# Chunk 5's phased convolution taps between the two halves of the last output pair, and chunk 7's VectorE taps less tied to chunk 6

## The chip, the cores and the metric

One core of a Trainium2 chip runs the whole program. The core has a matrix engine (TensorE, PE in the profile), three elementwise engines (VectorE or DVE, ScalarE or ACT, GpSimd or POOL) and queues that issue transfers: nearly all loads are issued, in order, by SP's queue, a few by ACT's. The metric is the time of one execution on the device, in microseconds, as a median over several executions. Each engine works through its own instruction list in order and waits on semaphores where an operand or a buffer isn't ready.

## The reference

The program is a two-layer decoder trunk in float32 on 512 tokens of 1024 channels. Layer 0 has a causal Conformer convolution module, layer 1 differential attention; each is followed by a SwiGLU feed-forward part and a gated per-layer embedding. Only the convolution module of layer 0 matters here:

```
a = x @ w_pw1 + b_pw1                       # 1024 -> 2048
u = a[..., :1024] * sigmoid(a[..., 1024:])
u = depthwise causal conv of u over 31 tokens, per channel, + dw_b
u = silu(layer_norm(u, ln_g, ln_b))
h = x + u @ w_pw2 + b_pw2
```

## The kernel before, in words

**Tiling.** Channels are cut into 8 chunks of 128, one chunk to the 128 partitions, with the 512 tokens along the free side. A float32 product is made of three matmuls on a high and a low part of each operand (lines 167 to 169), so one half of an output pair, which sums over 8 chunks of the input, is 24 matmuls of 128x512.

**Output pairs.** The loop over c makes, for each chunk, a pair of halves: the gate half `pg` and the linear half `pa`. VectorE scales both by the norm's row (line 583 for the gate, line 589 for the other), ScalarE takes the sigmoid (line 584), and VectorE multiplies them to the convolution's input (line 595 for phased chunks, line 603 for the others).

**Three ways to make the 31 taps.** A tap is a shifted copy of the input times one weight per channel.
- Chunks 1, 3, 5 and 6 are phased: the input goes to DRAM (line 420) and back (line 424, four loads) so that four tokens in four phases lie on the partitions, and 72 matmuls of 128x128 (line 457) with prepared matrices make all taps. The matrices come by line 437 (groups 0 and 1), line 443 (groups 2 and 3) and line 447 (the last lag of all groups). Then ScalarE copies the sum out (line 465), it goes to DRAM (line 467, ACT's queue) and back in token order (line 470, four loads on SP's queue), and VectorE adds the bias and the shift (line 475): the chunk's output y.
- Chunks 0, 2 and 4 are done by VectorE (lines 505 and 508) and, for some taps, by ScalarE's products and GpSimd's sums (lines 495 and 496).
- Chunk 7 is done by all: 8 taps on TensorE (line 413, matrices by line 412), 7 by ScalarE and GpSimd (lines 492, 495, 496), 16 on VectorE (one at line 505 and 15 at line 508). VectorE adds the three at lines 512 and 514.

**Moments.** For the layer norm, every chunk's y is added to a sum (line 543) and its square (ScalarE, line 536) to another (line 541). After the last chunk, TensorE sums over the channels (line 198, four groups of matmuls), and a short chain over VectorE, GpSimd and ScalarE makes the norm's factors, which the second linear layer waits for. Between these stand products of the per-layer embedding (`factor`, 6 matmuls of 128x512 each), which need nothing of the convolution.

**What sets the order.** The program is written in one order, and an automatic scheduler then lists each engine's instructions by its own simulated times; `issue_after(x)` holds an instruction's place in the list behind that of x. Two tables say at which pair a chunk's phased taps are written: `BETWEEN[c]` puts them between the two halves of pair c, `BEHIND[c]` behind its second half.

```
        if c > 0:
            pg = half(wg) if c > 1 else g1
            for k in BETWEEN[c]:
                pe_taps(k)
            pa = half(wa) if c > 1 else a1
            for k in BEHIND[c]:
                pe_taps(k)
```

Tiles have fixed homes: a new tile waits until its home's last user is done. The matrices of phased chunks live in D0 to D5 (one buffer each) and C5 (two). Chunk 6 uses D3 and D4 for its group 0, D5 for the last lag, D0 and D1 for group 1; chunk 5 uses D0 and D1, D2, then D3 and D4; chunk 7's TensorE taps use D2 and D3.

Of the kernel before, what the change touches and what calls it, by code (L numbers as in the profile page):

```python
# [26 lines left out]
KW = 31  # L27
# [31 lines left out]
PHASED = (1, 3, 5, 6)  # L59


BETWEEN = ((), (0,), (), (1, 2), (), (3, 4), (), ())
BEHIND = ((), (), (), (), (), (), (5,), (6,))
NPH = 4
FG = P // NPH
LAGS = (KW + NPH - 2) // NPH + 1
# [25 lines left out]
def trunk(ctx, tc, xT, xtok, pT, wts, diag, dww, vec, rel, onehot, lamv, out):  # L92
# [9 lines left out]
    def sb(shape, tag, bufs, dt=F32):  # L102
        uid[0] += 1
        return pool.tile(shape, dt, tag=tag, name=f"{tag}_{uid[0]}", bufs=bufs)
# [17 lines left out]
    def col(name, i=0):  # L122
        a, _ = VEC[name]
        return vt[:, a + i : a + i + 1]
# [260 lines left out]
    last_shift = [None]  # L385
# [4 lines left out]
    def half(w):  # L390
        acc = mm()
        for k in range(NC):
            mm3(acc, wpart(w, k), norm.u[k], k == 0, k == NC - 1)
        return acc

    def wt(c, j):
        return dwt[:, c * KW + j : c * KW + j + 1]
# [4 lines left out]
    def pe_taps(c):  # L402

        acc = accs[c] = sc() if c < NC - 2 else mm()
        if c in PHASED:
            return phased_taps(c, acc)
        for j in range(PE_TAPS[c]):
            if j % 4 == 0:
                n = min(4, PE_TAPS[c] - j)
                dg = sb([P, 4, P], f"D{2 + j // 4}", 1)  # L410
                with after_weights(c):
                    nc.sync.dma_start(dg[:, :n], diag[TAPS.index((c, j)), :, :n])
            last_tap[0] = T.matmul(
                acc, dg[:, j % 4], ups[c][:, j : j + S], start=(j == 0), stop=(j == PE_TAPS[c] - 1)
            )
# [46 lines left out]
    def phased_out(c):  # L462

        o = big()
        last_out[0] = A.copy(o, accs[c])
        d = dram.tile([P, S], F32, tag=f"po{c}", name=f"po{c}")
        nc.scalar.dma_start(d, o)
        both_ = sb([P, 2, S], f"B{c}", 1)
        for g in range(NPH):
            nc.sync.dma_start(  # L470
                both_[g * FG : (g + 1) * FG, 1].rearrange("p (r n) -> p r n", r=NPH),
                bass.AP(d.tensor, d.offset + g * P, [[S, FG], [FG * S, NPH], [1, P]]),
            )
        tok = "p (n r) -> p n r"
        last_shift[0] = V.scalar_tensor_tensor(
            both_[:, 0].rearrange(tok, r=NPH), both_[:, 1].rearrange("p (r n) -> p n r", r=NPH), col("dw_b", c),
            shrow.rearrange(tok, r=NPH), ALU.add, ALU.add,
        )
        y[c] = both_[:, 0]

    def other_taps(c):
        if c in PHASED:
            return phased_out(c)
        up, acc = ups[c], accs[c]
        alone = c in ALONE
        tap = lambda j: up[:, j : j + S]
        a, b = PE_TAPS[c], PE_TAPS[c] + POOL_TAPS[c]
        pacc = wk()
        for j in range(a, b):
            if j == a:  # L490
                with tc.issue_after(last_out[0].ins) if alone else nullcontext():
                    A.activation(pacc, tap(j), AF.Identity, scale=wt(c, j), bias=col("dw_b", c))
            else:
                pr = sb([P, S], f"C{2 + j % 2}", 2)
                A.activation(pr, tap(j), AF.Copy, scale=wt(c, j))
                G.tensor_tensor(pacc, pacc, pr, ALU.add)  # L496
        yc = sb([P, 2, S], f"B{c}", 1)
        if c == 0:
            sums["acc"] = yc[:, 1]
        yc = yc[:, 0]  # L500
        sum_ = sc() if alone else acc
        if c == 0:
            V.tensor_scalar(sum_, tap(b), wt(c, b), None, ALU.mult)
        else:
            V.scalar_tensor_tensor(sum_, tap(b), wt(c, b), shrow, ALU.mult, ALU.add)
        for j in range(b + 1, KW):
            with tc.issue_after(last_shift[0].ins) if alone and j == KW - 4 else nullcontext():
                last_v_tap[0] = V.scalar_tensor_tensor(sum_, tap(j), wt(c, j), sum_, ALU.mult, ALU.add)  # L508
        if alone:
            moments(NC - 2)  # L510
        with tc.issue_after(last_sum[0].ins) if alone else nullcontext():
            V.tensor_tensor(yc, sum_, pacc, ALU.add)
        if alone:
            last_add[0] = V.tensor_tensor(yc, acc, yc, ALU.add)
        y[c] = yc
# [10 lines left out]
    def moments(c):  # L526
        if c == 0:
            t = tp()
            T.matmul(t, ones, y[0], start=True, stop=True)
            A.activation(shrow, t, AF.Copy, scale=-1.0 / P)  # L530
            V.scalar_tensor_tensor(y[0], t, -1.0 / P, y[0], ALU.mult, ALU.add)
            A.activation(sums["acc"], y[0], AF.Square)
            return
        sq = sums["sq"] = wk()
        with tc.issue_after(last_factor[0].ins) if c > NC - 3 else nullcontext():
            A.activation(sq, y[c], AF.Square)
        if c == NC - 1:
            return
        eng, at = (V, tc.issue_after(last_v_tap[0].ins)) if c == NC - 2 else (G, nullcontext())
        with at:  # L540
            last_sum[0] = eng.tensor_tensor(sums["acc"], sums["acc"], sq, ALU.add)
            if c > 1:
                eng.tensor_tensor(macc, y[1] if c == 2 else macc, y[c], ALU.add)
# [6 lines left out]
    for c in range(NC):  # L550
# [24 lines left out]
# [7 lines that stand above are left out]
# [18 lines left out]
        else:  # L600
            up = ups[c] = sb([P, S + PAD], "C0", 2)
            G.memset(up[:, :PAD], 0.0)
            V.scalar_tensor_tensor(up[:, PAD:], ta, col("b_pw1", c), tg, ALU.add, ALU.mult)
        for k in BETWEEN[c] + BEHIND[c]:
            other_taps(k)
# [22 lines left out]
    for m in range(5):  # L628
        factor(last_tap)
        if m == 1:  # L630
            last_factor[0] = last_copy[0]
    other_taps(NC - 1)
    moments(NC - 1)

# [838 lines left out]
```

## Time and profile before

| | us |
|---|---|
| median of 3 runs | 1249.22 |
| lowest and highest of them | 1247.81 and 1250.43 |
| the profiled execution's own time | 1246.65 |
| its span (first to last instruction) | 1244.8 |
| TensorE busy in it | 1231.8 |
| VectorE, ScalarE, GpSimd busy | 879.8, 623.7, 464.7 |

The profiled execution is 2.57 us faster than the median, and 1.85 us of it lie outside its span. Times in the profile count from the span's start. In a list of waits a row names who waited, for whom, the microseconds in total, how often, and the longest. In a timeline a row gives start, length, engine, line, what is written from what, and in brackets the idle time before it with what ended it. Buffer numbers are left out there.

### The profile page before, as it was taken

Reading aid. Unit: us, or ns where it says so; the run is one execution under the profiler, and the core shown is the slowest. Engines: PE = TensorE matmul, PEld = TensorE weight load, DVE = VectorE, ACT = ScalarE, POOL = GpSimd, SP = SyncE. Lnnn points to the kernel's source line nnn. Section 1 sums busy time; section 2 is a strip of 40 time slices with the busy share of each in tenths; the row PEclk is TensorE's granted clock in tenths of the full one; section 3 lists DMA queues with packets and bytes.
Section 4 is the critical chain, followed back from the end, with each engine's and each line's share of the span. In section 5 each row is a group of like instructions: output and inputs, shape, how many; then the busy total and the mean of one; then the engine's idle time right before and its main releaser. Section 6 shows DMA issues by size and latency. Waiting matters only on the chain.

```text
span 1244.8 us, 18364 instructions
## 1 busy us (share of the span) xinstructions
PE 1231.8 (99%) x7048; PEld 1078.6 (87%) x7048; DVE 879.8 (71%) x1244; ACT 623.7 (50%) x1098; POOL 464.7 (37%) x351
## 2 busy tenths in 40 slices
PE   9999999999999999999999999999999999999998
PEld 7887788888998899888888888788889998999887
DVE  5997866985895479547676876646966885588535
ACT  7742464433553255435666877735434552455432
POOL 0953442024670464133436645041026650552120
PEclk9999999999999999999999999999999999999999
DMA  9756214234233322334332331142233333232331
GB/s 328 226 179 189 82 54 121 92 98 127 88 100 118 102 86 78 109 104 153 130 116 63 112 94 34 52 150 87 90 127 90 103 113 111 83 102 86 105 98 68
DMA packets 50019, 138.44 MB, mean 111 GB/s; under 512 B 5731, under 2 KB 10851, under 8 KB 49932
## 3 DMA queue, kind: packets, MB, share of 16 engines
q1 hardware_dynamic: 47664, 133.71, 34.1%
q10 hardware_dynamic: 2268, 3.57, 1.0%
q8 instruction: 55, 0.90, 0.3%
q14 instruction: 32, 0.26, 0.1%
HBM read 130.94 MB, written 6.31 MB: 110 GB/s over the span
## 4 chain that ended last, share of the span: by engine, by line
PE 84%; DVE 7%; issue 4%; ACT 2%; POOL 2%; DMA 1%; SPq 0%; DVEq 0%; POOLq 0%; ACTq 0%
PE mm L167 26%; PE mm L168 25%; PE mm L169 25%; DVE wlo L782 2%; POOL wk L496 1%; PE mm L1188 1%; DVE sc L508 1%; DVE wlo L162 1%; PE sc L457 1%; PE sc L1155 1%; PE sc L1156 1%; DVE B L873 1%; PE mm L457 1%; PE tp L1175 1%; PE tp L1109 1%
## 5 line engine op out<-in xcount | busy, mean ns | idle before, releaser
L160 ACT CAST whi<-wraw 128x1024 fp32r<-128x1024 f32 (+1 forms) x139 | 141.2, 1024 | 219.8 <-PE mm L169 110.3
L162 DVE TENSOR_TENSOR wlo<-wraw,whi 128x1024 fp32r<-128x1024 f32 (+1 forms) x135 | 174.2, 1296 | 81.9 <-ACT whi L160 81.1
L167 PE MATMUL mm<-A,wlo 128*128 128x512 f32 (+1 forms) x552 | 214.0, 388 | 0.1
L168 PE MATMUL mm<-A,whi 128*128 128x512 f32 (+1 forms) x552 | 213.4, 387 | 0.0
L169 PE MATMUL mm<-A,whi 128*128 128x512 f32 (+1 forms) x552 | 211.0, 388 | 0.0
L167 PE MATMUL mm<-B,wlo 128*128 128x512 f32 x352 | 137.0, 389 | 0.0
L168 PE MATMUL mm<-B,whi 128*128 128x512 f32 x352 | 137.0, 389 | 0.0
L169 PE MATMUL mm<-B,whi 128*128 128x512 f32 x352 | 135.6, 389 | 0.0
L228 POOL TENSOR_TENSOR acc<-acc,wk 128x512 f32<-128x512 f32 x35 | 60.3, 1724 | 189.8 <-ACT wk L227 189.2
L168 PE MATMUL mm<-C,whi 128*128 128x256 f32 x448 | 126.8, 283 | 0.0
L167 PE MATMUL mm<-C,wlo 128*128 128x256 f32 x448 | 126.8, 283 | 0.0
L169 PE MATMUL mm<-C,whi 128*128 128x256 f32 x448 | 126.8, 283 | 0.0
L169 PEld LDWEIGHTS mm<-A,whi 128*128 128x128 f32 x552 | 103.6, 188 | 22.3 <-DVE A L206 1.1
L167 PEld LDWEIGHTS mm<-A,wlo 128*128 128x128 f32 x552 | 103.8, 188 | 21.7 <-DVE h L1319 0.5
L168 PEld LDWEIGHTS mm<-A,whi 128*128 128x128 f32 x552 | 103.8, 188 | 20.5
L782 DVE TENSOR_TENSOR wlo<-A,whi 128x1024 fp32r<-128x1024 f32 x60 | 107.5, 1802 | 19.7 <-ACT whi L781 19.7
L781 ACT CAST whi<-A 128x1024 fp32r<-128x1024 f32 x60 | 62.9, 1048 | 54.6 <-PE mm L169 43.8
L791 POOL TENSOR_TENSOR A<-wraw 128x512 f32<-128x512 f32 x16 | 23.7, 1482 | 169.8 <-DMA wraw<-in_wts 147.0
L791 POOL TENSOR_TENSOR A<-A 128x512 f32<-128x512 f32 x16 | 24.6, 1536 | 165.3 <-DMA A<-in_wts 162.6
L168 PEld LDWEIGHTS mm<-C,whi 128*128 128x128 f32 x448 | 86.0, 192 | 0.2
L167 PEld LDWEIGHTS mm<-C,wlo 128*128 128x128 f32 x448 | 86.0, 192 | 0.2
L169 PEld LDWEIGHTS mm<-C,whi 128*128 128x128 f32 x448 | 86.0, 192 | 0.0
(324 smaller groups left out, 3057.1 us busy)
## 6 DMA issues: line engine op xcount, KB each, us to landing
wraw<-in_wts SPq DMA_DIRECT2D x159, 512.0 KB, 3.6
A<-in_wts SPq DMA_DIRECT2D x32, 512.0 KB, 3.6
wraw<-in_wts SPq DMA_DIRECT2D x16, 384.0 KB, 3.1
D<-in_diag SPq DMA_DIRECT2D x22, 256.0 KB, 4.5
C<-in_diag SPq DMA_DIRECT2D x16, 256.0 KB, 4.7
h<-in_xT SPq DMA_DIRECT2D x8, 256.0 KB, 4.7
B<-in_xtok SPq DMA_DIRECT2D x4, 512.0 KB, 7.2
rest<-h SPq DMA_DIRECT2D x8, 256.0 KB, 2.6
```

Source lines behind the costliest of these rows:

```text
L160: A.copy(hi[:, cut], raw[:, cut])
L162: eng.tensor_tensor(lo[:, cut], raw[:, cut], f(hi[:, cut]), ALU.subtract)
L167: T.matmul(acc, al, bh, start=first, stop=False, **kw)
L168: T.matmul(acc, ah, bh, start=False, stop=False, **kw)
L169: return T.matmul(acc, ah, bl, start=False, stop=last, **kw)
L228: self.last = self.eng.tensor_tensor(self.acc, self.acc, sq, ALU.add)
L457: last_tap[0] = T.matmul(acc[:, g * P : (g + 1) * P], w, ups[c][:, g, LEAD - m : LEAD - m + P], start=(m == 0), stop=(m == LAGS - 1),)
L496: G.tensor_tensor(pacc, pacc, pr, ALU.add)
L508: last_v_tap[0] = V.scalar_tensor_tensor(sum_, tap(j), wt(c, j), sum_, ALU.mult, ALU.add)
L781: A.copy(hi, src)
L782: V.tensor_tensor(lo, src, f(hi), ALU.subtract)
L791: G.tensor_tensor(s[:, 0], r1[:, 0], r1[:, 1], ALU.add)
```

## The change

Chunk 5's phased taps leave the place behind pair 6 and are written between the two halves of pair 7. Of chunk 7's 15 taps at line 508, formerly the last four were held behind chunk 6's shift (line 475); now only the last one is.

```
-BETWEEN = ((), (0,), (), (1, 2), (), (3, 4), (), ())
-BEHIND = ((), (), (), (), (), (), (5,), (6,))
+BETWEEN = ((), (0,), (), (1, 2), (), (3, 4), (), (5,))
+BEHIND = ((), (), (), (), (), (), (), (6,))
...
         for j in range(b + 1, KW):
-            with tc.issue_after(last_shift[0].ins) if alone and j == KW - 4 else nullcontext():
+            with tc.issue_after(last_shift[0].ins) if alone and j == KW - 1 else nullcontext():
                 last_v_tap[0] = V.scalar_tensor_tensor(sum_, tap(j), wt(c, j), sum_, ALU.mult, ALU.add)
```

Here is what the scheduler makes of it at three places. The first is TensorE around the start of chunk 5's taps. `sc_1003` and `sc_1047` are chunk 5's sum before and now, `mm_1085` and `mm_1022` the gate half of pair 7. Before:

```order
L169 MATMUL mm_1085<-A_33_141,whi_942 128x512
L167 MATMUL mm_1085<-A_34_146,wlo_943 128x512
L168 MATMUL mm_1085<-A_34_146,whi_942 128x512
L457 MATMUL sc_1003<-C_162_867,D_187_1004 128x128 x4
L457 MATMUL sc_1003<-C_162_867,D_188_1006 128x128 x4
L457 MATMUL sc_1003<-C_162_867,D_189_1008 128x128
```

Now:

```order
L167 MATMUL mm_1022<-A_40_172,wlo_943 128x512
L168 MATMUL mm_1022<-A_40_172,whi_942 128x512
L169 MATMUL mm_1022<-A_40_172,whi_942 128x512
L457 MATMUL sc_1047<-C_162_867,D_193_1048 128x128 x4
L457 MATMUL sc_1047<-C_162_867,D_194_1050 128x128 x4
L457 MATMUL sc_1047<-C_162_867,D_195_1052 128x128
```

The scheduler had let 5 of the gate half's 24 matmuls go ahead of chunk 5's taps; now all 24 do, and the 72 taps follow, and then the linear half of pair 7 and chunk 6's taps as before. The number of matmuls is the same.

The second place is VectorE from chunk 4's last sum (line 512) to chunk 6's shift (the last row). `B_199` and `B_213` are chunk 5's output before and now, `B_215` chunk 6's; `sc_1306` is chunk 7's sum. Before:

```order
L512 TENSOR_TENSOR B_176_915<-sc_832,wk_883 128x512
L583 TENSOR_TENSOR big_1188<-mm_1085,rb_273 128x512
L475 SCALAR_TENSOR_TENSOR B_199_1075<-B_199_1075,vec_63,shrow_190 128x512
L589 TENSOR_TENSOR big_1189<-mm_1110,rb_273 128x512
L603 SCALAR_TENSOR_TENSOR C_213_1194<-big_1189,vec_63,big_1188 128x512
L505 SCALAR_TENSOR_TENSOR sc_1306<-C_213_1194,C_31_133,shrow_190 128x512
L508 SCALAR_TENSOR_TENSOR sc_1306<-C_213_1194,C_31_133,sc_1306 128x512 x11
L475 SCALAR_TENSOR_TENSOR B_215_1201<-B_215_1201,vec_63,shrow_190 128x512
```

Now:

```order
L512 TENSOR_TENSOR B_176_915<-sc_832,wk_883 128x512
L589 TENSOR_TENSOR big_1179<-mm_1100,rb_273 128x512
L603 SCALAR_TENSOR_TENSOR C_211_1184<-big_1179,vec_63,big_1178 128x512
L505 SCALAR_TENSOR_TENSOR sc_1306<-C_211_1184,C_31_133,shrow_190 128x512
L508 SCALAR_TENSOR_TENSOR sc_1306<-C_211_1184,C_31_133,sc_1306 128x512 x5
L475 SCALAR_TENSOR_TENSOR B_213_1191<-B_213_1191,vec_63,shrow_190 128x512
L508 SCALAR_TENSOR_TENSOR sc_1306<-C_211_1184,C_31_133,sc_1306 128x512 x8
L475 SCALAR_TENSOR_TENSOR B_215_1201<-B_215_1201,vec_63,shrow_190 128x512
```

Chunk 5's shift has moved from ahead of pair 7's linear half into the middle of chunk 7's taps; the gate half's line 583 has moved ahead of line 512, among chunk 4's taps. Two taps instead of four stand behind chunk 6's shift.

The third place is SP's queue, from the write of chunk 6's input to chunk 5's return. `D_204`, `D_205`, `D_207`, `D_208` and the C tiles by line 443 are chunk 6's matrices before; `D_202`, `D_203` (its group 0), `D_205`, `D_206` (group 1) and `C_207`, `C_208` are the same ones now. `D_225` and `D_226` are for chunk 7's TensorE taps. Before:

```order
L437 DMA D_207_1142<-in_diag 128x512
L420 DMA pi_1063<-big_1061 128x512
L437 DMA D_208_1144<-in_diag 128x512
L156 DMA wraw_1452<-in_wts 128x1024
L437 DMA D_204_1136<-in_diag 128x512
L424 DMA C_197_1065<-pi_1063 32x4x128 x4
L437 DMA D_205_1138<-in_diag 128x512
L443 DMA C_209_1146<-in_diag 128x512 x2
L443 DMA C_210_1149<-in_diag 128x512 x2
L412 DMA D_225_1228<-in_diag 128x512
L470 DMA B_199_1075<-po_1073 32x4x128 x4
L412 DMA D_226_1234<-in_diag 128x512
```

Now:

```order
L420 DMA pi_1010<-big_1008 128x512
L156 DMA wraw_1452<-in_wts 128x1024
L424 DMA C_189_1012<-pi_1010 32x4x128 x4
L437 DMA D_205_1132<-in_diag 128x512
L437 DMA D_206_1134<-in_diag 128x512
L437 DMA D_202_1126<-in_diag 128x512
L437 DMA D_203_1128<-in_diag 128x512
L443 DMA C_207_1136<-in_diag 128x512 x2
L443 DMA C_208_1139<-in_diag 128x512 x2
L412 DMA D_225_1228<-in_diag 128x512
L412 DMA D_226_1234<-in_diag 128x512
L470 DMA B_213_1191<-po_1189 32x4x128 x4
```

Chunk 6's four D matrices now stand together behind the four loads of its input, group 1's ahead of group 0's, and chunk 5's return stands behind both loads for chunk 7. On ScalarE's list, which is not shown, chunk 5's copy (line 465) stood ahead of the square of chunk 4's output (line 536) and now stands behind it; the write to DRAM (line 467) follows the first of chunk 7's products (line 495); and the square of chunk 5's output stands directly ahead of chunk 6's copy (line 465) and of chunk 7's line 492.

## Prediction

> **What bounds the kernel now.** I read the page's busy times first (TensorE 1231.8 of a span of 1244.8 us), then the list of what TensorE waited for over the whole program, largest first:
>
> ```profile
> PE sc L457 <- DMA C<-pi: 3.0, 1, 3.0
> PE tp L142 <- POOL ident masks.py:199: 1.5, 1, 1.5
> ...
> PE tp L660 <- ACT wk L657: 0.7, 1, 0.7
> ```
>
> TensorE is the bound nearly everywhere, and its longest single wait is the one at phased taps (line 457) for an input that comes back from DRAM. So I asked next where that wait stands: TensorE's timeline around it.
>
> ```profile
> 100.66 0.39 PE L167 MATMUL mm<-A,wlo 128*128 128x512 f32 x1
> ...
> 101.56 0.39 PE L168 MATMUL mm<-A,whi 128*128 128x512 f32 x1
> 104.90 0.55 PE L457 MATMUL sc<-C,D 128*128 128x128 f32 x1 [2.95 <-DMA C<-pi]
> ...
> 114.49 0.48 PE L169 MATMUL mm<-A,whi 128*128 128x512 f32 x1
> ...
> 118.91 0.39 PE L167 MATMUL mm<-A,wlo 128*128 128x512 f32 x1
> ...
> 124.35 4.18 PE L457 MATMUL mm<-C,D 128*128 128x128 f32 x36
> ...
> 132.38 7.04 PE L413 MATMUL mm<-C,D 128*128 128x512 f32 x16
> ```
>
> It is chunk 5, behind the five gate matmuls that start at 100.66 to 101.56; 19 more of that half stand ready behind the waiting taps. The wait costs more than its length, as windows show (length, TensorE's busy time and its matmuls, granted clock, share and rate of the transfers):
>
> ```profile
> 101.90:104.90 3.00, 0.05 (x1) 0.98 0.78 150
> 104.90:106.00 1.10, 1.10 (x5) 0.50 0.59 194
> ...
> 107.00:108.00 1.00, 1.00 (x6) 0.50 0.01 4
> 108.00:109.00 1.00, 1.00 (x11) 0.92 0.71 227
> ...
> 154.00:155.00 1.00, 1.00 (x4) 1.00 0.00 0
> ```
>
> After the gap the clock is at half until about 108. After the 0.7 us gap at 153 (third row of the waits) it stays at 1.00.
>
> **What the change takes away.** Matmuls of 512 columns start 0.227 us apart (118.91 to 124.35 for 24 of them), so the taps could have begun at 101.56 + 0.23 = 101.79 and began at 104.90: 3.11 us. Chunk 5's 72 taps take 114.49 - 104.90 = 9.59 us, chunk 6's equal 72 take 132.38 - 124.35 = 8.03 us: 1.56 us more for the half clock. With the whole gate half ahead, the taps start at 101.79 + 19 x 0.227 = 106.1, later than the 104.9 at which their input was there, without a gap: **4.67 us** go. The matmuls are the same in number. TensorE then stands 4.67 us earlier at the linear half (end 119.8 for 124.5), at chunk 6's taps (119.7 for 124.35) and onward, if nothing else is late.
>
> [...]
>
> **What must come earlier now.** Three chains are less covered than before.
>
> *Chunk 6's input and matrices.* SP's queue, and times to landing (last number) of single transfers from 110 to 113 us:
>
> ```profile
> 110.07 0.33 SPq L420 DMA_DIRECT2D pi<-big  x1
> ...
> 111.12 0.33 SPq L156 DMA_DIRECT2D wraw<-in_wts  x1
> ...
> 112.11 1.75 SPq L424 DMA_DIRECT2D C<-pi  x4
> ```
>
> ```profile
> D<-in_diag SPq DMA_DIRECT2D x1, 256.0 KB, 2.6
> wraw<-in_wts SPq DMA_DIRECT2D x1, 512.0 KB, 5.3
> D<-in_diag SPq DMA_DIRECT2D x1, 256.0 KB, 6.3
> C<-pi SPq DMA_DIRECT2D x1, 64.0 KB, 6.0
> ```
>
> VectorE's list up to line 595 is unchanged, so the write of chunk 6's input stays at 110.07 and its loads at 112.11 to 113.9. They landed by about 119.5 (113.5 + 6.0) with 1 MB queued ahead (two D tiles of 256 KB and one weight); now the weight alone, 0.5 MB, is ahead: I take about 117.5. The four D loads follow from 113.9, the one needed last for group 0 behind the weight's landing, with which it shares a semaphore (111.12 + 5.3 at most): issued by 116 at the latest, needed at 119.7 + 4 x 0.11 = 120.1. The two D rows bound its landing: 2.6 us gives 118.6 and no wait, 6.3 gives 122.3 and a wait of 2.2 us. The queue is shorter than that of the 6.3 row and longer than that of the 2.6 row; I take a wait of 0.2 us. Groups 2 and 3 have 4 us more.
>
> *Chunk 5's return.* VectorE's timeline, in which chunk 5's shift is the row of 126.15:
>
> ```profile
> 126.15 1.12 DVE L475 SCALAR_TENSOR_TENSOR B<-B,vec,shrow 128x512 f32<-128x512 f32 x1 [6.35 <-DMA B<-po]
> 127.19 0.68 DVE L589 TENSOR_TENSOR big<-mm,rb 128x512 f32<-128x512 f32 x1
> ...
> 129.28 1.66 DVE L505 SCALAR_TENSOR_TENSOR sc<-C,C,shrow 128x512 f32<-128x512 f32 x1
> 130.97 8.67 DVE L508 SCALAR_TENSOR_TENSOR sc<-C,C,sc 128x512 f32<-128x512 f32 x11
> 139.68 1.85 DVE L475 SCALAR_TENSOR_TENSOR B<-B,vec,shrow 128x512 f32<-128x512 f32 x1
> ...
> 146.46 0.69 DVE L514 TENSOR_TENSOR B<-mm,B 128x512 f32<-128x512 f32 x1
> ```
>
> VectorE stood 6.35 us before chunk 5's shift and held the linear half of pair 7 (line 589) behind it, 2.7 us after TensorE had ended it. Now line 589 runs at 119.9 and line 505 at 119.9 + 2.1 = 122.0. From line 505 to the end of line 514 the old list took 147.15 - 129.28 = 17.87 us; the new one has the same work and chunk 5's shift in it, 1.12: 141.0, if neither return is waited for. The returns:
>
> ```profile
> 127.36 0.63 ACT L536 ACTIVATE wk<-B 128x512 f32<-128x512 f32 x1 [4.69 <-DVE B L475]
> ...
> 132.59 0.59 ACT L465 COPY big<-mm 128x512 f32<-128x512 f32 x1 [0.74 <-PE mm L457]
> 133.07 0.81 ACT L492 ACTIVATE wk<-C,vec,C 128x512 f32<-128x512 f32 x1
> 133.20 0.33 ACTq L467 DMA_DIRECT2D po<-big  x1
> ```
>
> ```profile
> 122.68 1.75 SPq L470 DMA_DIRECT2D B<-po  x4
> ...
> 135.19 1.75 SPq L470 DMA_DIRECT2D B<-po  x4
> ```
>
> Chunk 5's copy now stands on ScalarE behind chunk 4's square and its write behind chunk 7's first product, which needs line 603: it goes out at about 122.6. Chunk 6's write took 135.19 - 133.20 = 2.0 us to landing, so chunk 5's loads go at 124.7, also past the load for chunk 7's D3, which waits only for chunk 6's first taps (121). Chunk 5's shift began 126.15 - 122.68 = 3.5 us after its loads: now 128.2. Line 505 and five taps of 0.79 us end at 127.65, so VectorE waits 0.5 us.
>
> *Chunk 6's return and chunk 7's sum.* Behind chunk 5's shift (end 129.3) ScalarE's list has that chunk's square (0.63, line 536), then chunk 6's copy (0.59): the write goes at 130.5, the loads at 132.5, and landing 4.3 us after (139.5 for 135.19 as the upper bound, since VectorE didn't wait there) gives 136.8, against eight taps that end at 135.6: 1.2 us. So chunk 7's output comes at 141.0 + 0.5 + 1.2 = 142.7. GpSimd's six sums are behind the same copy:
>
> ```profile
> 127.41 1.28 POOL L543 TENSOR_TENSOR acc<-acc,B 128x512 f32<-128x512 f32 x1 [5.84 <-DVE B L475]
> 128.65 1.74 POOL L541 TENSOR_TENSOR B<-B,wk 128x512 f32<-128x512 f32 x1
> 133.96 8.67 POOL L496 TENSOR_TENSOR wk<-wk,C 128x512 f32<-128x512 f32 x6 [3.58 <-ACT wk L492]
> ```
>
> Line 492 ends at 131.3, chunk 5's two moments on GpSimd (1.28 + 1.74) at 132 to 132.4, and 132.4 + 8.67 = 141.1 is in time for line 512 (141.2). TensorE asks for chunk 7's output here:
>
> ```profile
> 147.87 1.06 PE L198 MATMUL sc<-ones,B 128*128 128x128 f32 x8
> ```
>
> That was 0.7 us after it was ready; now it asks at 147.87 - 4.67 = 143.2, 0.5 us after 142.7. The cover is thin: if the returns are as quick as chunk 5's, the wait is 0; if both are slow, several us (the rivals). I take 0.3 us.
>
> Behind these sums every list is the old one and starts from TensorE, so the rest moves as a block. Sum: 4.67 - 0.2 - 0.3 = 4.2 us. The profiled execution of 1246.65 (span 1244.8 and 1.85 around it) would take 1242.5; the median shown lies 2.57 above the profiled execution, and from it the forecast is **1245.0**.
>
> **The rivals.**
>
> *The half clock isn't paid in every execution.* The runs lie between 1247.81 and 1250.43, more than 1.56 apart, so the profile may not show the usual case. Then 3.11 - 0.5 = 2.6 us go: 1246.6. For it: the gap is the only one of its length, so the trace has no second case. Against it: the profiled execution paid it and was the fastest of the four. [...]
>
> *Chunk 6's matrices become the new wait.* The D row of 6.3 us gives 2.2 us: 4.67 - 2.2 - 0.3 = 2.2, so 1247.0. For it: six 256 KB loads and the input now go out in one block. Against it: 0.5 MB less is queued ahead of the input.
>
> *Chunk 7's sum eats the gain.* A lateness of 1.5 to 3 us beyond 143.2 leaves nothing to 3 us: about 1248.5.
>
> *Slower: the two returns follow each other.* Chunk 6's copy now waits for chunk 5's shift, by ScalarE's order, so slow transfers add up. Slow rows of their kinds:
>
> ```profile
> po<-big ACTq DMA_DIRECT2D x1, 256.0 KB, 4.1
> B<-po SPq DMA_DIRECT2D x1, 64.0 KB, 4.3
> ```
>
> With 4.1 for both writes, 4.3 behind the last issue for the first return and 6.0 (the row of C<-pi, same size and kind) for the second: chunk 5's shift at 126.7 + 1.3 + 4.3 = 132.3, chunk 6's write at 134.6, its last load landing at 138.7 + 1.3 + 6.0 = 146.0, and from there 5.9 (the old 147.15 - 139.68 less two taps) make 152. TensorE would wait 8.8 us and then run at half clock for 1.56 more: 10.4 - 4.67 = 5.7 slower, 1254.9. It decides from a lateness of 3.1 us, where 3.1 + 1.56 equals the gain. Against it: these rows are from the crowded stretches, and traffic around 125 to 136 is light.
>
> **How the numbers follow.** Chances: forecast 0.58 (own range 1243.6 to 1246.2), half clock not usual 0.12, matrices 0.15, gain eaten 0.09, slower 0.06. A difference of 0.2%, 2.5 us, is about what a measurement of this kernel can tell from no change, so faster means below 1246.7: all of the forecast and two thirds of the two cases behind it, whose waits reach down to none, 0.76; same 0.18; slower 0.06. The range reaches from 1243.2 (no waits at all, 1244.6, and the spread of a median) to 1247.9, beyond the matrices' case, and leaves out most of the last two.
>
> **What would show it.** Right: no wait of TensorE at chunk 5's taps, 72 of them in 8.0 us from about 106.1, granted clock 1.00 throughout 100 to 160, pair 7's linear half ending near 119.8, chunk 5's shift near 128, line 198 starting near 141.4 instead of 146.08. Wrong: a wait at chunk 6's taps for D or C<-pi; a wait at line 198 for line 514; or a difference that arises behind 155, where I expect none.

## The result, and the profile after

| kernel | median, us | lowest to highest | runs |
|---|---|---|---|
| before | 1248.80 | 1247.54 to 1250.71 | 6 |
| changed | 1243.91 | 1243.17 to 1245.44 | 6 |

The change makes the kernel faster by 4.9 us: the ratio is 0.9963, with a 95% interval of 0.9952 to 0.9975. The prediction was 1245.0, in a range of 1243.2 to 1247.9. The profiled execution of the changed kernel is the slowest of its six, 1245.44 us with a span of 1243.6, while that of the kernel before, 1246.65, was quicker than each of its six timed runs. So the two traces must be compared by what happens in them and not by their ends: 1243.6 against 1244.8 looks like 1.2 us.

The list of what TensorE waited for in the changed kernel, between 95 and 165 us:

```profile
PE sc L457 <- DMA C<-pi: 1.3, 1, 1.3
PE mm L457 <- DMA D<-in_diag: 1.2, 1, 1.2
PE tp L660 <- ACT wk L657: 1.2, 1, 1.2
```

The wait of 3.0 us at chunk 5's taps is 1.3 now, a wait for chunk 6's matrices is new, and the third one, for the factors of the norm, grew from 0.7 to 1.2. TensorE's timeline gives their places (chunk 5's taps, chunk 6's taps, chunk 7's taps, the first and the third sum of the moments):

```profile
108.00 4.26 PE L457 MATMUL sc<-C,D 128*128 128x128 f32 x36 [1.26 <-DMA C<-pi]
...
122.94 4.26 PE L457 MATMUL mm<-C,D 128*128 128x128 f32 x36 [1.20 <-DMA D<-in_diag]
...
131.05 7.04 PE L413 MATMUL mm<-C,D 128*128 128x512 f32 x16
...
144.74 1.05 PE L198 MATMUL sc<-ones,acc 128*128 128x128 f32 x8
...
146.56 1.16 PE L198 MATMUL sc<-ones,B 128*128 128x128 f32 x8
```

In the trace of before, chunk 5's taps and the first sum stood here:

```profile
104.90 5.81 PE L457 MATMUL sc<-C,D 128*128 128x128 f32 x36 [2.95 <-DMA C<-pi]
...
146.08 1.05 PE L198 MATMUL sc<-ones,acc 128*128 128x128 f32 x8
```

The first 36 records of either chunk's taps take 4.26 us now; chunk 5's took 5.81 at half clock. The windows around chunk 5's taps (length, TensorE's busy time, the busy times of its weight loads and the other engines, and then the granted clock) show that the short gap no longer slows what follows:

```profile
107.00:108.00 1.00, 0.00 (x1) 0.03 (x1) 0.00 (x0) 0.00 (x0) 0.00 (x0) 1.00 0.77 181
108.00:109.00 1.00, 1.00 (x9) 1.00 (x10) 0.71 (x1) 0.00 (x0) 0.00 (x0) 1.00 0.84 332
109.00:110.00 1.00, 1.00 (x12) 1.00 (x11) 1.00 (x2) 0.56 (x2) 0.45 (x1) 1.00 0.16 61
```

Why is there a gap at all, with the whole gate half ahead of the taps? SP's queue tells it: the write of chunk 5's input, its loads, the write of chunk 6's input, its loads, and four matrices.

```profile
99.10 0.33 SPq L420 DMA_DIRECT2D pi<-big  x1
...
102.58 1.80 SPq L424 DMA_DIRECT2D C<-pi  x4
...
113.16 0.34 SPq L420 DMA_DIRECT2D pi<-big  x1
...
115.19 2.53 SPq L424 DMA_DIRECT2D C<-pi  x4
117.82 1.80 SPq L437 DMA_DIRECT2D D<-in_diag  x4
```

In the execution of before, the loads of chunk 5's input were issued at 100.16 and chunk 6's input was written at 110.07; here it is 102.58 and 113.16, although nothing ahead of them was changed. This execution ran about 2.4 to 3.1 us late there. VectorE's timeline shows the same, at the shifts of chunks 3, 5 and 6 (line 475) and chunk 7's last sum (line 514):

```profile
108.29 1.12 DVE L475 SCALAR_TENSOR_TENSOR B<-B,vec,shrow 128x512 f32<-128x512 f32 x1 [1.81 <-DMA B<-po]
...
131.53 1.11 DVE L475 SCALAR_TENSOR_TENSOR B<-B,vec,shrow 128x512 f32<-128x512 f32 x1 [1.47 <-DMA B<-po]
...
139.64 1.85 DVE L475 SCALAR_TENSOR_TENSOR B<-B,vec,shrow 128x512 f32<-128x512 f32 x1 [0.79 <-DMA B<-po]
...
145.82 0.69 DVE L514 TENSOR_TENSOR B<-mm,B 128x512 f32<-128x512 f32 x1
```

The first of these, chunk 3's shift, stood here in the trace of before:

```profile
105.20 1.11 DVE L475 SCALAR_TENSOR_TENSOR B<-B,vec,shrow 128x512 f32<-128x512 f32 x1 [1.14 <-DMA B<-po]
```

It began at 105.20 before and at 108.29 here, 3.09 us later; all the same, line 198 begins at 144.74 instead of 146.08. From chunk 3's shift, which lies ahead of everything the change touches, to line 198 it is 146.08 - 105.20 = 40.88 us before and 144.74 - 108.29 = 36.45 now: **4.43 us less**. I use this distance as a yardstick for the runs below, since it takes an execution's own lateness out. It is one execution of each kernel, and where TensorE has slack it absorbs some of that lateness; it is a reading aid, and the verdicts go by the timed runs.

The stall on VectorE went the same way. It stood 6.35 us before chunk 5's shift, with pair 7's product behind it; now 1.47.

### The profile page after: what moved, and what is told of

The parts are those of the page before. It is cut to its first block, busy times and chain, and to the rows that moved or that the text cites. A ratio compares the mean times of both kernels' runs of the same rounds, so it can differ in the third digit from the quotient of the medians.

```text
span 1243.6 us, 18365 instructions
## 1 busy us (share of the span) xinstructions
PE 1230.1 (99%) x7048; PEld 1077.2 (87%) x7048; DVE 879.4 (71%) x1244; ACT 624.8 (50%) x1098; POOL 467.5 (38%) x351
## 4 chain that ended last, share of the span: by engine, by line
PE 84%; DVE 7%; DMA 4%; issue 3%; ACT 1%; SPq 0%; POOL 0%; ACTq 0%; DVEq 0%
PE mm L167 26%; PE mm L168 26%; PE mm L169 26%; DMA wraw<-in_wts 2%; DVE wlo L162 2%; PE mm L1188 1%; DVE sc L508 1%; DVE wlo L782 1%; PE sc L1155 1%; PE sc L1156 1%; DMA B<-in_xtok 1%; PE tp L1175 1%; PE mm L457 1%; PE tp L1109 1%; PE mm L413 1%
## 5 line engine op out<-in xcount | busy, mean ns | idle before, releaser
L791 POOL TENSOR_TENSOR A<-wraw 128x512 f32<-128x512 f32 x16 | 26.3, 1643 | 165.8 <-DMA wraw<-in_wts 143.4
```

The lines of the kernel that those rows point to most:

```text
L791: G.tensor_tensor(s[:, 0], r1[:, 0], r1[:, 1], ALU.add)
```

## The experiments

All were timed beside the kernel before on the same chip, in four groups. The kernel before lies between 1247.35 and 1248.57 in them, so ratios are compared rather than medians of different groups. The ratios are as the comparison of each group gives them and not the quotient of the two medians.

| run | median, us | lowest to highest, runs | before beside it | ratio, 95% interval |
|---|---|---|---|---|
| e1 tables only | 1246.26 | 1244.17 to 1248.33, 12 | 1248.57 | 0.9982, 0.9972 to 0.9991 |
| e2 hold only | 1247.80 | 1245.91 to 1250.14, 11 | 1248.57 | 0.9998, 0.9989 to 1.0007 |
| e3 filled gap | 1247.50 | 1246.68 to 1248.85, 11 | 1248.57 | 0.9996, 0.9987 to 1.0006 |
| e3b short fill | 1247.45 | 1245.90 to 1248.74, 11 | 1247.38 | 1.0002, 0.9994 to 1.0011 |
| e3c fill and order | 1247.33 | 1245.66 to 1248.45, 11 | 1247.35 | 0.9997, 0.9988 to 1.0006 |
| e11 fill and hold | 1247.12 | 1245.38 to 1248.60, 12 | 1248.05 | 0.9994, 0.9985 to 1.0003 |
| e4 group 0 first | 1243.99 | 1243.00 to 1244.62, 5 | 1248.57 | 0.9967, 0.9955 to 0.9978 |
| e5 write first | 1243.16 | 1241.97 to 1244.21, 8 | 1247.38 | 0.9970, 0.9960 to 0.9980 |
| e7 products early | 1242.39 | 1240.31 to 1242.55, 6 | 1247.38 | 0.9964, 0.9952 to 0.9976 |
| e8 shift late | 1241.25 | 1240.77 to 1241.79, 5 | 1247.38 | 0.9959, 0.9947 to 0.9971 |
| changed, again | 1243.49 | 1242.25 to 1244.29, 5 | 1247.35 | 0.9965, 0.9953 to 0.9978 |
| e8, again | 1241.72 | 1240.72 to 1242.57, 5 | 1247.35 | 0.9952, 0.9938 to 0.9965 |

### The two edits apart

e1 moves the taps and keeps the old hold:

```
-BETWEEN = ((), (0,), (), (1, 2), (), (3, 4), (), ())
-BEHIND = ((), (), (), (), (), (), (5,), (6,))
+BETWEEN = ((), (0,), (), (1, 2), (), (3, 4), (), (5,))
+BEHIND = ((), (), (), (), (), (), (), (6,))
```

> Only chunk 5's taps are moved between the halves of pair 7; the last four of chunk 7's VectorE taps stay held behind chunk 6's shift, so the shift stands after 11 of the 15 taps instead of 13. In the changed kernel's trace that shift waited 0.79 us for its return with 13 taps ahead, and chunk 7's output was ready when TensorE asked for it. Theory (the move of the taps brings the gain, and the cover of chunk 7's sum is used up): the shift waits 0.79 + 2 x 0.79 = 2.4 us, chunk 7's output is up to 1.6 us later, TensorE waits about 1.2 us at line 198: 1243.9 + 1.2 = 1245.1, still 3.7 below the kernel before. Rival (chunk 7's sum has cover to spare, the hold is idle): 1243.9.

e2 keeps the tables and changes the hold:

```
-            with tc.issue_after(last_shift[0].ins) if alone and j == KW - 4 else nullcontext():
+            with tc.issue_after(last_shift[0].ins) if alone and j == KW - 1 else nullcontext():
```

> Only the hold is loosened (the shift of chunk 6 after 13 of chunk 7's taps instead of 11), chunk 5's taps stay behind pair 6. In the trace of before VectorE did not wait at that shift, and TensorE not at line 198. Theory: no change, 1248.8 within 1. Rival (the loosened hold brings a good part of the gain by itself): 1246 or less.

The hold alone gives nothing (0.9998). The tables alone give 0.9982, about half of the whole change's 0.9963, and the two intervals (0.9972 to 0.9991 and 0.9952 to 0.9975) hardly overlap: taken across the two groups, about 2 us are left for the hold once the taps have moved. I had expected a wait of 1.2 us at line 198 in e1 and 1245.1 us; line 198 did not wait there, and the time was 1246.26. TensorE in e1, chunk 5's taps and chunk 6's:

```profile
106.67 4.18 PE L457 MATMUL sc<-C,D 128*128 128x128 f32 x36
...
122.44 5.88 PE L457 MATMUL mm<-C,D 128*128 128x128 f32 x36 [2.11 <-DMA C<-in_diag]
```

No wait at chunk 5's taps: the gap of before is gone, as the prediction's first step has it. The half clock has moved: a wait of 2.11 us for matrices and then 5.88 us for the 36 records at chunk 6's taps. VectorE in e1, chunk 6's shift:

```profile
139.73 1.70 DVE L475 SCALAR_TENSOR_TENSOR B<-B,vec,shrow 128x512 f32<-128x512 f32 x1 [3.84 <-DMA B<-po]
```

VectorE stands 3.84 us before that shift with four taps of chunk 7 and four sums behind it; with the new hold two of these four taps run ahead of the shift. With the old order (e2) VectorE has no wait there to fill, so the same edit does nothing. That this is how the hold gains is argued and not shown: VectorE's sum of line 543 ended at 145.06 in e1, before line 198 began at 145.89, and what TensorE lost up to there it lost at chunk 6's taps. Part of e1's distance is that half clock: its four runs with a mean clock of 0.998 average 1247.2 us, the eight others 1245.4, and none of the changed kernel's eleven is below 0.999. Whether the hold keeps the clock up there was not tried. By the yardstick e1 gains only 40.88 - (145.89 - 106.13) = 1.1 us in its profiled execution.

e2's profile holds the gap of before in a larger size:

```profile
106.08 5.88 PE L457 MATMUL sc<-C,D 128*128 128x128 f32 x36 [3.96 <-DMA C<-pi]
```

### Is the half clock a cost of its own?

e3 keeps the order of before and lets TensorE do idle work in the gap, so that the clock stays up (1.00 there in its profile). The product of the filler is thrown away.

```
+FILL = 27
...
+                    started[0] = mm()
+                    with tc.manual_schedule(engines={T.engine}):
+                        for n in range(5):
+                            gate_matmul(pairs[NC - 1][1], n)
+                        fill = tp()
+                        for _ in range(FILL):
+                            T.matmul(fill[:, 0:P], ident, ones, start=True, stop=True)
+                        pe_taps(k)
```

> The kernel before with 27 matmuls of 128x128 that nobody reads between the fifth gate matmul of pair 7 and chunk 5's taps: about 3.0 us of work in the gap, so that the wait stays and only the idleness goes. The matmuls, their operands and VectorE's list are those of before; on SP's queue chunk 6's D matrices move behind its input, where they have 5 us to spare. Theory (the half clock behind the gap costs 1.56 us in the usual execution): 1248.8 - 1.5 = 1247.3, 72 taps in 8.0 us, granted clock 1.00 at 100 to 115. Rival (the profiled execution was unusual there, and the wait alone is the price): 1248.8, with the taps as long as before in only some executions.

The size was wrong: a float32 matmul of 128x128 stands twice in the records, at 0.11 us each, so 27 of them took 6.19 us, longer than the gap. (So the 72 that stand for a chunk's taps are records too, of 36 matmuls in the program.) The clock was 1.00 from 100 to 160 and the ratio 0.9996, which tells nothing of the half clock's price. e3b has `FILL = 14`.

> The kernel before with 14 matmuls of idle work (recorded as 28, some 3.1 us by the 0.1115 us of a record in the run with the longer filler) put ahead of chunk 5's phased taps, where TensorE waited 2.95 to 3.96 us for their input. The filler's product is thrown away. My theory, that the half clock behind that gap is a cost of its own of about 1.5 us which goes when the gap is filled: no stretch below clock 1.00 at 105 to 110, the 36 first records of taps in about 4.2 us rather than 5.9, and 1247.1 us beside 1248.6 for the kernel before. Rival, that the half clock does not occur in most executions, or that what comes behind the taps waits anyway: 1248.6, within 0.2% of the kernel before.

The 28 records took 3.29 us, no stretch from 100 to 160 was below 1.00, the first 36 taps took 4.26 us and chunk 6's taps began at 123.61 instead of 124.35. The total did not move (1.0002). In its profile ScalarE's copy of chunk 5's sums stood behind chunk 4's square, at 120.36 instead of 114.77, and chunk 7's taps waited 1.27 us. e3c takes that away by holding the square behind the write:

```
-        with tc.issue_after(last_factor[0].ins) if c > NC - 3 else nullcontext():
+        held = last_factor[0] if c > NC - 3 else outs[c + 1] if c == 4 else None
+        with tc.issue_after(held.ins) if held else nullcontext():
             A.activation(sq, y[c], AF.Square)
```

> The kernel before with the short filler again, and with chunk 4's square on ScalarE held behind the write to DRAM of chunk 5's sums. In the first run with the short filler no stretch was at half clock and chunk 6's taps began at 123.61 us rather than 124.35, but ScalarE's copy of chunk 5's sums had moved behind chunk 4's square (120.36 us rather than 114.77), chunk 5's shift ended 3.7 us later, and chunk 7's taps waited 1.27 us; the total had not moved. With the hold ScalarE has the order of the kernel before. My theory, that the half clock is a cost of its own: no wait at chunk 7's taps, and about 1.2 us below the kernel before (ratio 0.999). Rival, that the half clock costs nothing in most executions: within 0.05% of the kernel before, with the same waits.

The copy was back at 114.56 and the wait at chunk 7's taps gone, and the total still did not move (0.9997). TensorE in e3c (lines 603, 471 and 199 are the filler, the taps and the moments' sums):

```profile
102.21 3.29 PE L603 MATMUL tp<-ones,ident 128*128 128x128 f32 x28
106.24 4.26 PE L471 MATMUL sc<-C,D 128*128 128x128 f32 x36 [0.74 <-DMA C<-pi]
...
147.10 1.16 PE L199 MATMUL sc<-ones,acc 128*128 128x128 f32 x8 [1.06 <-DVE acc L558]
```

Line 198 (199 here) now waits 1.06 us for VectorE's sum. e11 adds the hold to e3c, in case VectorE's four taps behind chunk 6's shift were what it waited for:

> The run with the short filler and the order restored, and with the change's other edit too (only chunk 7's last tap on VectorE behind chunk 6's shift). The filler alone took the half clock away and gained nothing (ratio 0.9997); in its profile line 198 waited 1.06 us for the sum with chunk 6's output. The hold alone gained nothing either (0.9998). My theory, that the half clock is a cost of its own and that what it gave back was eaten at line 198, where VectorE has four taps left behind chunk 6's shift: with one tap left there, the wait at line 198 is gone or under 0.3 us, and the time is 1.0 to 1.5 us below the kernel before (ratio 0.9988 to 0.9992). Rival, that the half clock costs nothing that another wait in the returns through DRAM would not cost: within 0.05% of the kernel before, with a wait at line 198 of about 1 us again.

The ratio is 0.9994, with an interval that holds both theories, but the profile decides against mine: line 198 waits 1.08 us again. VectorE and TensorE in e11, chunk 5's shift and line 198:

```profile
130.44 1.12 DVE L489 SCALAR_TENSOR_TENSOR B<-B,vec,shrow 128x512 f32<-128x512 f32 x1 [8.69 <-DMA B<-po]
...
145.43 1.14 DVE L489 SCALAR_TENSOR_TENSOR B<-B,vec,shrow 128x512 f32<-128x512 f32 x1
```

```profile
107.18 4.26 PE L471 MATMUL sc<-C,D 128*128 128x128 f32 x36 [1.78 <-DMA C<-pi]
...
148.67 1.16 PE L199 MATMUL sc<-ones,acc 128*128 128x128 f32 x8 [1.08 <-DVE acc L558]
```

VectorE stands 8.69 us before chunk 5's shift and does not wait again before line 198: with chunk 5's shift ahead of pair 7's product, VectorE's list from there to line 198 is full, and its start is set by chunk 5's return. In before's profile this second chain ends right under TensorE's. VectorE's row of line 543, whose sum line 198 reads first:

```profile
144.47 0.68 DVE L543 TENSOR_TENSOR acc<-acc,B 128x512 f32<-128x512 f32 x1
```

It ended at 144.47 + 0.68 = 145.15, 0.93 us before line 198 began at 146.08. So what TensorE wins at chunk 5's taps in the old order is worth at most 0.9 us as long as chunk 5's return does not come earlier too, and nothing where it is later, as in all four of these runs (chunk 5's shift at 128.87 to 130.44, against 126.15 and, in e2, 127.35).

The return does not follow TensorE there. ScalarE's copy of chunk 5's sums and its write to DRAM, in before and then in e3c:

```profile
114.77 0.58 ACT L465 COPY big<-sc 128x512 f32<-128x512 f32 x1 [6.86 <-PE sc L457]
118.58 0.33 ACTq L467 DMA_DIRECT2D po<-big  x1
```

```profile
114.56 0.59 ACT L479 COPY big<-sc 128x512 f32<-128x512 f32 x1 [5.30 <-PE sc L471]
119.17 0.33 ACTq L481 DMA_DIRECT2D po<-big  x1
```

The write went out 3.2 us after the copy had ended in before and 4.0 us in e3c. In before, e2, e3c and e11 it left 0.07 to 0.08 us after the landing of a load of SP's queue to which the trace gives the same semaphore (118.51, 118.67, 119.09 and 120.24: one of chunk 6's input loads in the first two, its first matrices in the filled runs). Then its own way, up to the loads behind it, took 6.1 and 6.0 us in e3c and e11 (to 125.25 and 126.34) against 4.1 and 4.9 in before and e2. In the filled runs SP's list has the matrices of chunk 6 in one block behind its input, as in the changed kernel, rather than spread from 107 on; whether this block is what slows the write was not tried apart. **The half clock's own price therefore stays open.** What is shown is that it did not bound the old order alone.

### What stands next behind the change

e4 issues the first half of chunk 6's D matrices ahead of the second:

```
-                    nc.sync.dma_start(two[m], diag[i + 2 * g + m])
+                    with tc.issue_after(lead[0].ins) if c == 6 and g else nullcontext():
+                        ld = nc.sync.dma_start(two[m], diag[i + 2 * g + m])
+                    if g == 0:
+                        lead[0] = ld
```

> The changed kernel with chunk 6's two D matrices of group 0 loaded ahead of those of group 1; nothing else moves. In the changed kernel's trace chunk 6's taps waited 1.20 us for a D matrix, and chunk 7's output came just as TensorE asked for it. Theory (chunk 7's sum is the next bound): the D wait falls to about 0.4, but TensorE then asks 0.8 earlier for an output that is not earlier, and waits there: 1243.9 - 0.2 = 1243.7. Rival (the D wait is on the path alone): 1243.9 - 0.9 = 1243.0.

TensorE in e4, chunk 6's taps and line 198:

```profile
120.83 4.26 PE L460 MATMUL mm<-C,D 128*128 128x128 f32 x36 [0.46 <-DMA D<-in_diag]
...
143.86 1.16 PE L198 MATMUL sc<-ones,acc 128*128 128x128 f32 x8 [1.07 <-DVE acc L546]
```

The wait for matrices shrank to 0.46 us, a wait of 1.07 appeared at line 198, and the time is that of the changed kernel (0.9967 for 0.9963): the returns through DRAM stand next (VectorE waits 2.21 us for chunk 5's there and 0.94 for chunk 6's). e5 adds that ScalarE writes chunk 5's and 6's sums out before it takes the squares of chunks 4 and 5 (the edit of e3c, with `c > 3` for `c == 4`):

> The changed kernel with the first half of chunk 6's D matrices issued ahead of the second, and the squares of chunks 4 and 5 on ScalarE held behind the issue of the writes to DRAM of the sums of chunks 5 and 6. Theory, that what is next behind the change is the return of chunks 5 and 6 through DRAM: the writes go out 0.5 to 1 us earlier, the two shifts on VectorE end 0.5 to 1 us earlier, the wait of 1.07 us at line 198 shrinks to 0.5 or less, and the time is 1243.3 us beside 1244.0 of the run with the D matrices alone. Rival, that GpSimd's chain of six sums for chunk 7 ends last at that place anyway: within 0.3 us of 1244.0.

e7 also writes chunk 7's products and GpSimd's sums earlier, without their hold behind ScalarE's copy of chunk 6's sums:

```
-                with tc.issue_after(last_out[0].ins) if alone else nullcontext():
-                    A.activation(pacc, tap(j), AF.Identity, scale=wt(c, j), bias=col("dw_b", c))
+                A.activation(pacc, tap(j), AF.Identity, scale=wt(c, j), bias=col("dw_b", c))
...
+    early[NC - 1] = products(NC - 1)
     moments(NC - 3)
     pe_taps(NC - 1)
```

> The run with the writes first, and chunk 7's products on ScalarE and sums on GpSimd written ahead of chunk 6's way out and without their hold behind ScalarE's copy of chunk 6's sums. Theory, that both chains (the return and GpSimd's sums) meet at line 198: GpSimd's six sums end 2 us or more earlier, line 198 waits for nothing, and the time is 1242.9 us. Rival, that the products on ScalarE now stand in front of chunk 6's copy and its write, so that chunk 6's return is late: a wait of 1 to 3 us at line 198 for chunk 6's square, 1244 to 1246 us.

And e8 moves VectorE's shift of chunk 3 behind the product that makes chunk 6's input:

```
+        if c == 3:
+            later.append(shift)
+        else:
+            shift()
...
             phased_in(c, up)
+            if c == 6:
+                with tc.issue_after(made.ins):
+                    later.pop()()
```

> The run with the products early, and VectorE's shift of chunk 3 (line 475) placed behind the product that makes chunk 6's input (line 595), so that VectorE does not wait for chunk 3's return ahead of chunk 6's input. Theory, that the arrival of chunk 6's input and matrices still costs 1 to 2 us at its taps: the write of chunk 6's input goes out 2 to 4 us earlier than in the changed kernel (113.16 us there), no wait of 0.3 us or more is left at either chunk's taps, and the time is 1242.0 us. Rival, that nothing waits for it any more or that chunk 3's moments come late in its place: within 0.3 us of the run with the products early, or up to 1 us above it.

On one chip the three medians fall in turn, 1243.16, 1242.39 and 1241.25. e5's wait at line 198 is gone from its first sum and stands at 0.27 and 0.24 us at the second and third; in e7 and e8 there is none. Their intervals overlap, so each step's size is not established, and their ratios to the kernel before (0.9970, 0.9964 and 0.9959) are not clear of e4's 0.9967 or of the changed kernel's 0.9963: the shorter waits do not show in the time of any single step. The input's write in e8 went out at 110.40 against 113.16, but 111.15 in e7 without the edit: most of that difference is the execution's. Its loads left no earlier (114.05 and 113.29 in e8's two profiles, 113.17 in e7), so what the moved shift itself does is not shown. To set the end of the row against the changed kernel, both ran on one chip:

> The changed kernel once more, on the chip of the two other runs here. My theory, that its first profiled execution had chunk 6's input and matrices late because the work in front of them ran 2.4 to 3.1 us late there: in an execution with the write of chunk 5's input near 97 us, the wait at chunk 5's taps is gone and the wait for D matrices at chunk 6's taps is 0.5 us or less; 4 to 5 us below the kernel before. Rival, that these waits belong to the change whatever the execution: again 1.2 us at both places.

> The run with the shift late once more, beside the changed kernel on one chip. My theory, that its three edits shorten the executions of the changed kernel: no wait of 0.3 us or more on TensorE between 100 and 146 us, and 1.5 to 2.5 us below the changed kernel (a ratio to the kernel before of about 0.995). Rival, that the difference of the two medians so far lay between two chips: within 0.7 us of the changed kernel.

The changed kernel again gave 1243.49 beside 1247.35, and e8 1241.72: **1.8 us better than the changed kernel**, and only its two slowest runs of five (1242.49 and 1242.57) lie above the fastest of the other's five (1242.25). The intervals of their ratios, 0.9938 to 0.9965 and 0.9953 to 0.9978, still overlap. TensorE in e8's second profile, chunk 5's taps, chunk 6's, chunk 7's and line 198, without a wait:

```profile
106.18 4.18 PE L462 MATMUL sc<-C,D 128*128 128x128 f32 x36
...
119.71 4.18 PE L462 MATMUL mm<-C,D 128*128 128x128 f32 x36
...
127.75 7.03 PE L415 MATMUL mm<-C,D 128*128 128x512 f32 x16
141.44 1.05 PE L198 MATMUL sc<-ones,acc 128*128 128x128 f32 x8
```

The changed kernel's second profile, chunk 5's taps, chunk 6's taps and line 198, and SP's write of chunk 5's input:

```profile
107.04 4.26 PE L457 MATMUL sc<-C,D 128*128 128x128 f32 x36 [0.58 <-DMA C<-pi]
...
121.76 4.26 PE L457 MATMUL mm<-C,D 128*128 128x128 f32 x36 [0.97 <-DVE B L512]
...
143.56 1.05 PE L198 MATMUL sc<-ones,acc 128*128 128x128 f32 x8
```

```profile
98.07 0.33 SPq L420 DMA_DIRECT2D pi<-big  x1
```

The write is 1.38 us later than in before's profile (96.69), and the wait at chunk 5's taps 0.58: less late and less wait than in the first profile (2.41 and 1.26), as my theory had it. In e1 (written at 97.17) the same taps did not wait at all. The wait at chunk 6's taps hardly fell (0.97 after 1.20), against my 0.5, so the rival is half right. This row names VectorE's line 512, which ended at 120.79 + 0.69 = 121.48; the first matrices of group 0, issued at 117.62, landed 3.8 us later, at 121.4. The two are 0.1 us apart, so this profile does not tell which of them the taps waited for; in the first profile, and in e1 and e4, the row names a load of matrices. The yardstick gives 143.56 - 107.32 = 36.24, or 4.64 us less than before.

## Why the prediction was right

**The number is in part luck.** The mechanism held: the gap of 3.11 us is down to waits of 1.26 and 0.58, the half clock behind it and VectorE's stall of 6.35 us are gone, and the time fell. The sizes did not. In the changed kernel's two profiles line 198 begins 1.34 and 2.52 us earlier than in before's, where 4.7 were forecast, and a wait at chunk 6's taps for D, named as a sign of being wrong, came at 1.20 us. The terms of 0.2 and 0.3 us, and the 0 at chunk 5's taps, were too small by some 2 to 3 us together. What made up for it is a term that was held constant: the 2.57 us by which the usual execution of before lies above the profiled one. The changed kernel's profiled executions lie 1.53 and 0.45 us above their medians, not below. So part of those 2.57 us seems to have gone with the change, and two errors of opposite sign bring 4.2 near the measured 4.9.

**The gap and the half clock, 4.67 us: held, and the gap was larger in other profiles.** With all 24 gate matmuls ahead, chunk 5's taps began without a wait in e1, e4, e5, e7 and e8 (106.00 to 106.85, predicted 106.1), and in the two profiles of the changed kernel they waited 0.58 and 1.26 us. The granted clock is 1.00 from 100 to 160 in both. The gap of 3.11 us was a small one: the wait was 3.96 us in e2, and from the filler's start to the taps it was 105.72 - 101.74 = 3.98 us in e3b, 106.24 - 102.21 = 4.03 in e3c and 107.18 - 102.11 = 5.07 in e11. That can be a part of what the usual execution loses. It may not be all: 34 of the 79 runs of before that stand beside the experiments have a mean clock of 0.996 or 0.997, lower than any profiled run of any kernel here, and average 1248.9 us against 1246.9 of the other 45. No profile shows such an execution, so where it loses its time is open.

**Chunk 6's input and matrices, 0.2 us: too small.** "The write of chunk 6's input stays at 110.07" failed: 113.16 and 112.21. Its place in the list did stay; the list itself ran late in these executions, and its lateness reaches SP's whole queue. The four D matrices began to be issued at 117.82 and 116.72, where the last one needed was to be out by 116, and TensorE waited 1.20 and 0.97 us. The block is also larger than the prediction has it: eight loads of 256 KB, not six. e4 shows that about half a microsecond of the wait is the order of issue.

**Chunk 5's return: right in its order, late in its time.** The shift began at 131.53 and 130.30 us, not 128.2, and VectorE waited 1.47 and 1.20 for it where I had 0.5. Two terms were off. VectorE's line 589 ran at 122.36 and 121.40 instead of 119.9, behind chunk 4's taps, which were as late as the shift of chunk 3; and the write to DRAM took 128.21 - 124.59 = 3.6 and 127.01 - 123.63 = 3.4 us to its loads, where I had taken 2.0 from chunk 6's. In e1 the write went out at 122.44, as forecast (122.6), and the shift still began at 130.15. The stall of 6.35 us is nevertheless gone. I had treated that stall as what pair 7's half waited for; by the filled runs it is more, since the chain that follows it ended 0.93 us under TensorE's own, and moving TensorE alone gained nothing in them. That the change could gain more, because the same edit also takes chunk 5's shift out of pair 7's way, fits this and is not shown apart.

**Chunk 7's sum, 0.3 us: it was 0.5 to 0.6, and at another place.** Its last sum ended at 145.82 + 0.69 = 146.51, when line 198's third group asked at 146.56: no wait there. But VectorE has 2.35 us of weight parts behind that sum before it starts the norm's factors, so the lateness comes out at line 660: from line 198 to line 660 it was 153.60 - 146.08 = 7.52 us before and 152.90 - 144.74 = 8.16 now, and the wait for ScalarE there is 1.19 for 0.69. e7 and e8 have 0.69 again. Whether it reaches the end can't be read: see the distances behind line 198 below.

**The hold.** I had counted its effect only within VectorE's new list and given it no price of its own. It is nothing alone and, across two groups of runs, about 2 us with the tables; its way of gaining is not shown.

**Behind line 198 no difference is seen**, as forecast: from its start to the span's end it is 1244.8 - 146.08 = 1098.7 us before, 1098.9 and 1098.6 in the changed kernel's two profiles. Over all fourteen profiles it lies between 1096.8 and 1100.1, so less than a microsecond or so can't be told there. Line 198 began at 144.74 and 143.56 rather than at 141.4, which e5 and e8 reach (141.23 and 141.44): the 141.4 was the time of an execution as early as the profiled one.

**The rivals.** That the half clock is not usual fell: 54 of the 79 runs of before have a mean clock of 0.996 to 0.998, where the three profiled runs with one such stretch have 0.998, 0.998 and 0.999 and those without have 0.999 or 1.000. It is not in every execution, though: three runs have 1.000, and 0.999 tells neither way, for the clock also falls to 0.50 in the last microseconds of the span (in e1, e4 and the changed kernel's second profile; in its first one from 1242.4 to the end at 1243.6, behind TensorE's last matmul). That the matrices become the new wait came in part, at 1.0 to 1.2 us of the 2.2 that it named, and in full (2.11) in e1. That chunk 7's sum eats the gain came with 0.6 of its 1.5 to 3. The two returns following each other cost 1.47 + 0.79 us on VectorE in place of 8.8 on TensorE; without the new hold (e1) it was 2.24 + 3.84, the nearest that any run came to it.

## What to carry to other kernels

A stall on TensorE for one return through DRAM and a stall on VectorE for the next one of the same chunk belonged together here: filling the first gained only what the other chain left, at most 0.9 us by before's profile and nothing in four runs. It is worth looking for an edit that takes the waiting step out of both lists. Before asking what a return will gain from an earlier engine, look at what its write really waits for; in before it left 0.07 us behind a load's landing and 3.2 us behind the copy. Before forecasting from one profile, look how far the arrival of the inputs varies between executions; a gap that is 3 us in a quick execution was 4 to 5 in others. After such a move, look at what the in-order queues now issue last, since the next waits lay in the order of loads and writes there (1.20 us at chunk 6's taps, and 0.46 with its first matrices ahead in e4).

## What the runs showed of the hardware

The clock fell to half after gaps on TensorE of 2.11 (e1), 2.95 (before) and 3.96 us (e2), and stayed at 1.00 after 0.58 to 1.78 us (1.26 and 1.20 in the changed kernel, 1.78 in e11). e1's windows, in which the third column from the end is the granted clock:

```profile
122.00:123.00 1.00, 0.56 (x5) 0.59 (x6) 0.96 (x2) 1.00 (x3) 1.00 (x1) 1.00 1.10 297
123.00:124.00 1.00, 1.00 (x11) 1.00 (x10) 0.96 (x2) 1.00 (x3) 0.40 (x1) 0.89 0.95 322
124.00:125.00 1.00, 1.00 (x7) 1.00 (x7) 0.96 (x2) 0.92 (x2) 0.00 (x0) 0.50 1.03 395
...
127.00:128.00 1.00, 1.00 (x10) 1.00 (x10) 0.88 (x2) 0.00 (x0) 0.00 (x0) 0.90 0.09 28
```

TensorE works from 122.44 on, and the clock falls at about 123.8, more than a microsecond later; it is 0.50 in the three windows from 124 to 127 and back by 127.2, so about 3.4 us were at half. How long a gap must be for this was not tried apart: the shortest with it was 2.11 us, the longest without it 1.78.

A second thing was the size of the lateness between executions of one kernel: the write of chunk 5's input left at 96.69 to 99.10 us in the fourteen profiles, though no kernel here changes what stands ahead of it, while TensorE's place moved less (it was ready for chunk 5's taps at 106.00 to 106.85 wherever the whole gate half went ahead). What makes the early stage late in one execution and not in another was not tried.
